# RWKV pair scores of a two-layer mixer trunk: ScalarE copies and a GpSimd select in place of VectorE's masked copies

## The chip, the core and the metric

The kernel runs on one core of a Trainium2 chip. The metric is the device time of one execution in microseconds, the median of several runs. A core has five engines that work side by side and wait for each other by semaphores: TensorE (PE in the rows, its weight loads PEld), VectorE (DVE), ScalarE (ACT), GpSimd (POOL) and SyncE (SP). Each engine takes its own instructions strictly in the order in which they stand in its queue, and DMAs are issued from the queues of SP and ACT here. An instruction that waits therefore holds up everything behind it on its engine.

## What is computed

The reference is a trunk of two layers on 256 positions of width 1024. Each layer normalises its input, projects it into the head groups of four token mixers (stick-breaking attention, RWKV-7, block attention, HGRN2), gates and sums their outputs, projects once more, and ends in a SwiGLU feed-forward part. The change touches RWKV-7 alone, whose recurrence is

```python
def step(state, inp):
    r_t, w_t, k_t, v_t, a_t, b_t = inp
    sa = jnp.einsum('bhvk,bhk->bhv', state, a_t)
    state = (state * w_t[:, :, None, :] + sa[..., None] * b_t[:, :, None, :]
             + v_t[..., None] * k_t[:, :, None, :])
    return state, jnp.einsum('bhvk,bhk->bhv', state, r_t)
```

for four heads of 64. The kernel computes it in two chunks of 128 positions. In a chunk, every pair of an earlier position s and a later position t has a score for each head: two tables, LB from b and LK from k, each against a (pairs s < t) and against r (pairs s <= t). Pairs outside these triangles count as zero. From LB a triangular system is solved, first in blocks of 16.

## The kernel before

All matrix products of the projections are made in three passes over a high and a low part: `split` (lines 127 to 129) makes the high part of a weight tile by a cast on ACT (`hi`) and the low part by a subtraction on DVE (`lo`). TensorE takes one weight tile of 128x1024 after another; four such pairs fit (`spl=4`), so a cast waits until TensorE has finished with the pair four tiles back.

The function `drive` interleaves the projections with two streams of mixer work by a planned TensorE clock: stream 0 is `rwkv`, stream 1 is `sba`, `moba` and `hgrn` in turn. The order on TensorE follows from that plan. On the other engines a scheduler sets the order from the dependences as it sees them.

Inside `rwkv` the part that matters runs like this, in each layer:

- `pair_scores` (line 534) is called four times: for LB of chunks 0 and 1, then LK of chunks 0 and 1. It makes eight small matmuls into two PSUM tiles `p1` (two buffers in all, so the next call's matmuls wait until the tiles before are read), two heads in each. A memset on GpSimd has zeroed the target `dst` (128 rows s, four heads, 256 columns: 128 for a, 128 for r), and line 542 lets DVE copy only the pairs in the triangle, by the 0/1 mask `armask`.
- `send` (line 547) writes the a half of LB to `flat` in HBM by a DMA from ACT's queue (line 548). Line 564, also from ACT's queue, reads the 16x16 diagonal blocks back as `xb` (tile `h`) when both writes have landed.
- Lines 570 to 594, on DVE, invert these blocks in `yb`. Line 599 writes `yb` to `tri` in HBM and line 602 reads it back spread over all partitions, both from ACT's queue. Line 602 waits until the write has landed.

At the same time TensorE runs the last projection of HGRN (`hgrn_proj`, function `use_n`, lines 809 to 813): two PSUM tiles `pa`, each emptied by a copy and a sigmoid on ACT (lines 810 and 811) and a product on DVE (line 812). There are three `pa` buffers. The gate unit that follows takes the third one and then needs the first of these two back, so its matmuls wait for line 812.

Of the kernel before, what the change touches and what calls it, by code (L numbers as in the profile page):

```python
# [15 lines left out]
OP = mybir.AluOpType  # L16
# [30 lines left out]
def trunk(ctx, tc, x, w_t, w_n, w_br, w_out, w_gu, w_dn, par, lora, rows, gains, consts, masks, out):  # L47
    nc = tc.nc
# [8 lines left out]
    def sb(tag, width, dt=F32):  # L57
        return mx.tile([128, width], dt, name=tag, tag=tag, bufs=NB[tag])

    def ps(tag):  # L60
        return psum.tile([128, 512], F32, name=tag, tag=tag, bufs=NB[tag])

    def g2d(t, a):
        return t.rearrange("p (a t) -> p a t", a=a)
# [4 lines left out]
    def over(t, n):  # L69
        return t[:, None, :].to_broadcast([128, n, t.shape[-1]])  # L70
# [3 lines left out]
    def mm(o, l, r, start=True, stop=True):  # L74
        n = 1
        for d in r.shape[1:]:
            n *= d
        m = l.shape[-1]
        pe[0] += max(m / 1.2, n / 2.4) if r.dtype == F32R else max(m / 0.6, n / 0.6)
        nc.tensor.matmul(o, l, r, start=start, stop=stop)  # L80
# [134 lines left out]
    armask = mk[:, 0:256]  # L215
# [220 lines left out]
    def head_sums(q, tag):  # L436
        p = ps(tag)
        for t in range(2):
            for hp in range(2):
                mm_cols(p[:, t * 4 + hp * 2:t * 4 + hp * 2 + 2], q[:, hp, t * 128:(t + 1) * 128], blk2)  # L440
        return p
# [4 lines left out]
    def hrow(a):  # L446
        return slice((a % 2) * 64, (a % 2) * 64 + 64)
# [17 lines left out]
    def rwkv(m, l, yT):  # L465
# [43 lines left out]
        p = head_sums(sq, "p1")  # L509
# [8 lines left out]
        p = ps("p1")  # L518
# [14 lines left out]

        def pair_scores(src, dst, c):
            p = [ps("p1"), ps("p1")]
            nc.gpsimd.memset(dst, 0.0)
            for a in range(4):
                hp = a // 2
                mm(p[a % 2][:, hp * 256:(hp + 1) * 256], src[hrow(a), hp, c * 128:(c + 1) * 128],
                   AR[hrow(a), 2 * hp + c].rearrange("p u t -> p (u t)"))  # L540
            for u in range(2):
                nc.vector.copy_predicated(dst[:, u::2], over(armask, 2), g2d(p[u], 2))  # L542

        flat = dram.tile([8, 128 * 129], F32, name="flat")
        tri = dram.tile([64, 256], F32, name="tri")
# [5 lines left out]
        for c in range(2):  # L551
            LB.append(g2d(sb("b1", 1024), 4))
            pair_scores(bn, LB[c], c)
            yield 1600
            send(c)
# [10 lines left out]
        for c in range(2):  # L566
            LK.append(g2d(sb("b1", 1024), 4))
            pair_scores(kh, LK[c], c)
            yield 3200
# [49 lines left out]
        for c in range(2):  # L619
            z5 = z[c].rearrange("p a (b u h) -> p a b u h", u=2, h=16)  # L620
            p = ps("p1")
# [4 lines left out]
        for c in range(2):  # L626
            p = ps("p1")
# [12 lines left out]
        p = [ps("p1"), ps("p1")]  # L640
# [6 lines left out]
        p = [ps("p1"), ps("p1")]  # L647
# [11 lines left out]
        for c in range(2):  # L659
            z6.append(g2d(sb("h1", 256), 4))  # L660
            p = ps("p1")
# [4 lines left out]
        for c in range(2):  # L666
            zs.append(g2d(sb("h1", 256), 4))
            p = ps("p1")
# [5 lines left out]
        for c in range(2):  # L674
            p = ps("p1")
# [6 lines left out]
        if l:  # L682
            p = ps("p1")
# [11 lines left out]
        p = ps("p1")  # L695
# [6 lines left out]
        p = ps("p1")  # L702
# [10 lines left out]
        p = head_sums(rx, "p1")  # L713
# [7 lines left out]
        p = ps("p1")  # L721
# [8 lines left out]
        for c in range(2):  # L730
            p = ps("p1")
# [9 lines left out]
            p = ps("p1")  # L741
# [3 lines left out]
            u = sb("h1", 256)  # L745
            nc.scalar.copy(u, p[:, 0:256])
            yield 1000
            if c == 0:
                p = ps("p1")
# [12 lines left out]
            p = ps("p1")  # L762
# [533 lines left out]
```

## Time and profile before

| | us |
|---|---|
| median of 3 runs | 926.57 (925.06 to 928.9) |
| the profiled execution | 930.03 |
| its span, first to last instruction | 928.2 |
| TensorE busy in the span | 910.3 |
| DVE, ACT, GpSimd busy | 651.4, 475.5, 83.8 |
| mean granted TensorE clock | 0.996 |

TensorE is the engine to look at: only what makes it wait, or what it waits for, can move the time. The second layer repeats the first one; in the place of this change it does so 452.6 us later (the write of `tri` is issued at 112.19 and at 564.75 us). The rows below come from the stretch around 80 to 120 us and its twin in the second layer.

### The profile page before, as it was taken

To read this page: it belongs to the slowest core of one execution; us is meant where nothing else is said; L and a number is where in the kernel's file an instruction comes from. 1 tells how busy PE (TensorE), PEld (TensorE's weight loads), DVE (VectorE), ACT (ScalarE), POOL (GpSimd) and SP (SyncE) were. 2 spreads that over 40 slices of the span, in tenths; PEclk is the share of its full clock that TensorE was granted. 3 is DMA by queue.
4 is the path that set the end of the run, shared out by engine and by line. 5 is a ranking of instruction groups with operands and counts; after the bars stand their busy time and mean duration, and the time that the engine had idled before them with its cause. 6 is when DMAs were issued, how large, how long until landed. Compare 5 with 4: busy or idle time off the path is not lost.

```text
span 928.2 us, 14996 instructions
## 1 busy us (share of the span) xinstructions
PE 910.3 (98%) x5902; PEld 761.5 (82%) x5902; DVE 651.4 (70%) x957; ACT 475.5 (51%) x726; POOL 83.8 (9%) x94
## 2 busy tenths in 40 slices
PE   8999899999999999999999998999999999999996
PEld 5999678778888888888889986767787888888885
DVE  5668877786766666677567778768678566666665
ACT  5564385445535545456445645644455345555453
POOL 3001100323000000000000201023130000000000
PEclk9999999999999999999999999999999999999999
DMA  8654454345864556568435444533368356666551
GB/s 302 204 159 137 130 175 136 114 147 166 256 220 134 183 183 184 182 206 272 155 114 161 159 140 127 186 103 115 119 208 264 114 181 204 185 182 201 181 181 46
DMA packets 50424, 158.11 MB, mean 170 GB/s; under 512 B 9393, under 2 KB 11953, under 8 KB 50354
## 3 DMA queue, kind: packets, MB, share of 16 engines
q1 hardware_dynamic: 43632, 155.19, 52.4%
q10 hardware_dynamic: 6722, 1.97, 0.9%
q8 instruction: 46, 0.75, 0.3%
q14 instruction: 24, 0.20, 0.1%
HBM read 154.91 MB, written 2.23 MB: 169 GB/s over the span
## 4 chain that ended last, share of the span: by engine, by line
PE 80%; DVE 10%; DMA 4%; issue 2%; ACT 2%; POOL 0%; SPq 0%; ACTq 0%; POOLq 0%; DVEq 0%
PE pa L80 56%; PE p L80 23%; DVE lo L129 2%; PE p L89 1%; PE pa L89 1%; DMA h<-flat 1%; DMA xr<-in_x_dram 1%; DVE b L542 1%; DMA flat<-b 1%; DVE xy L591 1%; DMA raw<-in_w_n_dram 1%; DMA lora<-in_lora_dram 1%; DMA raw<-in_w_gu_dram 1%; DVE b L867 1%; DVE b L965 1%
## 5 line engine op out<-in xcount | busy, mean ns | idle before, releaser
L129 DVE TENSOR_TENSOR lo<-raw,hi 128x1024 fp32r<-128x1024 f32 x268 | 331.0, 1240 | 153.6 <-ACT hi L128 150.6
L128 ACT CAST hi<-raw 128x1024 fp32r<-128x1024 f32 x268 | 279.2, 1048 | 225.5 <-PE pa L80 107.4
L80 PE MATMUL pa<-h,hi 128*128 128x256 f32 (+1 forms) x1280 | 277.9, 339 | 0.0
L80 PEld LDWEIGHTS pa<-h,hi 128*128 128x128 f32 x1280 | 215.9, 190 | 24.6 <-issue 2.0
L80 PE MATMUL pa<-hi,h 128*128 128x512 f32 x576 | 194.1, 402 | 4.6 <-DVE p L812 4.6
L80 PE MATMUL pa<-h,lo 128*128 128x256 f32 x960 | 179.9, 283 | 0.0
L80 PEld LDWEIGHTS pa<-h,lo 128*128 128x128 f32 x960 | 148.6, 191 | 7.0 <-issue 0.7
L80 PEld LDWEIGHTS pa<-hi,h 128*128 128x128 f32 x576 | 109.0, 189 | 31.5 <-DVE p L812 5.5
L80 PE MATMUL pa<-lo,h 128*128 128x512 f32 x288 | 113.6, 394 | 0.0
L80 PE MATMUL p<-hi,c 128*128 128x512 f32 (+1 forms) x352 | 113.4, 394 | 0.0
L80 PEld LDWEIGHTS p<-hi,c 128*128 128x128 f32 x352 | 66.1, 189 | 15.2 <-DVE c L129 0.6
L80 PE MATMUL p<-lo,c 128*128 128x512 f32 (+1 forms) x176 | 69.2, 393 | 0.0
L80 PEld LDWEIGHTS pa<-lo,h 128*128 128x128 f32 x288 | 54.5, 189 | 9.9
L263 POOL TENSOR_TENSOR rs<-rs,half 128x1 f32<-128x1 f32 x10 | 6.0, 597 | 471.6 <-DVE rs L262 471.6
L80 PE MATMUL pa<-hi,y 128*128 128x512 f32 x128 | 44.0, 399 | 0.1
L80 PE MATMUL p<-hi,b 128*128 128x512 f32 x128 | 41.4, 396 | 0.2 <-DVE b L129 0.2
L80 PEld LDWEIGHTS p<-lo,c 128*128 128x128 f32 x176 | 33.1, 188 | 6.8
L1033 POOL TENSOR_TENSOR p<-p,gt 128x512 f32<-128x512 f32 x16 | 30.9, 1953 | 39.4 <-DVE gt L1031 31.8
L340 DVE TENSOR_TENSOR gt<-gt,pa 128x256 f32<-128x256 f32 x80 | 33.2, 414 | 0.0
L128 ACT CAST c<-xy 128x512 fp32r<-128x512 f32 x20 | 12.4, 620 | 39.2 <-DVE xy L1136 39.2
L339 ACT COPY gt<-pa 128x256 f32<-128x256 f32 x80 | 29.3, 366 | 0.0
L80 PEld LDWEIGHTS pa<-hi,y 128*128 128x128 f32 x128 | 24.0, 188 | 6.3 <-issue 0.7
(276 smaller groups left out, 943.4 us busy)
## 6 DMA issues: line engine op xcount, KB each, us to landing
raw<-in_w_gu_dram SPq DMA_DIRECT2D x88, 512.0 KB, 3.9
raw<-in_w_n_dram SPq DMA_DIRECT2D x80, 512.0 KB, 3.6
raw<-in_w_dn_dram SPq DMA_DIRECT2D x44, 512.0 KB, 3.5
raw<-in_w_t_dram SPq DMA_DIRECT2D x40, 512.0 KB, 3.5
raw<-in_w_br_dram SPq DMA_DIRECT2D x16, 512.0 KB, 4.0
raw<-in_w_out_dram SPq DMA_DIRECT2D x16, 512.0 KB, 4.4
b<-in_gains_dram SPq DMA_DIRECT2D x4, 512.0 KB, 5.5
flat<-b ACTq DMA_DIRECT2D x4, 256.0 KB, 3.2
```

The costliest lines, as they stand in the source:

```text
L80: nc.tensor.matmul(o, l, r, start=start, stop=stop)
L89: nc.tensor.transpose(o, i, ident)
L128: a = nc.scalar.copy(dst[0], src)
L129: return a, (eng or nc.vector).tensor_tensor(dst[1], src, dst[0], op=OP.subtract)
L263: nc.gpsimd.tensor_tensor(dst, dst, half[:, :dst.shape[-1]], op=OP.pow)
L339: nc.scalar.copy(dst, p[:, 256:512])
L340: nc.vector.tensor_tensor(dst, dst, p[:, 0:256], op=OP.add)
L542: nc.vector.copy_predicated(dst[:, u::2], over(armask, 2), g2d(p[u], 2))
L591: nc.vector.tensor_tensor(pr[:, b, i], l4[:, b, i, None].to_broadcast(bc), r.to_broadcast(bc), op=OP.mult)
L867: nc.vector.tensor_tensor(qv, qv, t4[s, :, :, 0:1].to_broadcast([64, 2, 2 * nb, hb]), op=OP.mult)
L965: nc.vector.tensor_tensor_scan(kb, kb, reset[t][:, ::-1], 1.0, op0=OP.mult, op1=OP.add)
L1033: e.tensor_tensor(mg[f, t], mg[f, t], g, op=OP.add)
```

## The change

The memset goes. After the matmuls, ACT copies both PSUM tiles whole into `dst`, and GpSimd then goes over `dst` in place, once for the a half and once for the r half. Its select computes (column - row + u - 1) from the indices, keeps the element where that is not negative, and writes 0.0 elsewhere: s < t for u = 0, s <= t for u = 1.

```diff
         def pair_scores(src, dst, c):
             p = [ps("p1"), ps("p1")]
-            nc.gpsimd.memset(dst, 0.0)
             for a in range(4):
...
             for u in range(2):
-                nc.vector.copy_predicated(dst[:, u::2], over(armask, 2), g2d(p[u], 2))
+                nc.scalar.copy(dst[:, u::2], g2d(p[u], 2))
+            for u in range(2):
+                v = dst[:, :, u * 128:(u + 1) * 128]
+                nc.gpsimd.affine_select(v, v, [[0, 4], [1, 128]], OP.is_ge, 0.0, base=u - 1, channel_multiplier=-1)
```

In two layers with four calls each that is 16 masked copies on DVE and 8 memsets on GpSimd less, 16 copies on ACT and 16 selects on GpSimd more. Lines after 542 of the changed kernel are numbered two higher. TensorE's instructions and their order stay as they were; on the other engines the scheduler places some of the neighbours anew.

The first place is ACT's queue around the two writes of LB. `b1_953` is LB of chunk 0, `b1_1000` (in the changed kernel `b1_1001`) of chunk 1, `p1_...` their PSUM tiles, and what an instruction waits for stands in brackets. Before:

```order
L960 ACTIVATE b2_944<-b2_933 128x1024 [waits DVE_49]
L961 ACTIVATE b2_933<-b2_933 128x1024 [waits Activation_49]
L128 CAST hi_1113<-raw_1111 128x1024 [waits DMAHW4_49,PE_49]
L548 DMA flat_951<-b1_953 128x4x128 [waits DVE_49,Pool_49]
L548 DMA flat_951<-b1_1000 128x4x128 [waits DVE_49,Pool_49]
L796 COPY p_1022<-pa_916 128x512 [waits PE_49]
```

And in the changed kernel:

```order
L962 ACTIVATE b2_944<-b2_933 128x1024 [waits DVE_49]
L541 COPY b1_953<-p1_954 128x2x256 [waits PE_49]
L963 ACTIVATE b2_933<-b2_933 128x1024 [waits Activation_49]
L541 COPY b1_953<-p1_955 128x2x256 [waits PE_49]
L128 CAST hi_1115<-raw_1113 128x1024 [waits DMAHW4_49,PE_49]
L550 DMA flat_951<-b1_953 128x4x128 [waits Pool_49]
L541 COPY b1_1001<-p1_1002 128x2x256 [waits PE_49]
L541 COPY b1_1001<-p1_1003 128x2x256 [waits PE_49]
L550 DMA flat_951<-b1_1001 128x4x128 [waits Pool_49]
L798 COPY p_1024<-pa_916 128x512 [waits PE_49]
```

Both writes now wait for GpSimd, and the copies of chunk 1 stand behind the first of these waits.

The second place is ACT's queue around the write and the read of `tri`; `pa_1109` and `pa_1110` (in the changed kernel `pa_1111` and `pa_1112`) are the PSUM tiles of HGRN's last projection. Before:

```order
L128 CAST hi_1282<-raw_1280 128x1024 [waits DMAHW1_49,PE_49,Activation_49]
L128 CAST hi_1300<-raw_1298 128x1024 [waits DMAHW4_49,DVE_49,PE_49]
L128 CAST hi_1318<-raw_1316 128x1024 [waits DMAHW5_49,DVE_49,PE_49]
L599 DMA tri_952<-yb_118 64x256 [waits DVE_49]
L810 COPY p_1107<-pa_1109 128x256 [waits PE_49]
L811 ACTIVATE p_1108<-pa_1109 128x256
L602 DMA h1_1372<-tri_952 128x8x16 [waits DMAHW3_49,DMAHW1_49]
L810 COPY p_1107<-pa_1110 128x256 [waits PE_49]
```

And in the changed kernel:

```order
L128 CAST hi_1286<-raw_1284 128x1024 [waits DMAHW1_49,DVE_49,PE_49]
L541 COPY b1_1181<-p1_1182 128x2x256 [waits PE_49]
L541 COPY b1_1181<-p1_1183 128x2x256 [waits PE_49]
L601 DMA tri_952<-yb_118 64x256 [waits DVE_49]
L128 CAST hi_1304<-raw_1302 128x1024 [waits DMAHW4_49,PE_49,Activation_49]
L604 DMA h1_1376<-tri_952 128x8x16 [waits DMAHW0_49]
L128 CAST hi_1322<-raw_1320 128x1024 [waits DMAHW5_49,PE_49,Activation_49]
L812 COPY p_1109<-pa_1111 128x256 [waits PE_49]
L813 ACTIVATE p_1110<-pa_1111 128x256
L812 COPY p_1109<-pa_1112 128x256 [waits PE_49]
```

Two casts moved from before the write of `tri` to behind it, and the read of `tri` moved ahead of the first copy out of `pa`.

The third place is the end of the inversion on DVE, up to line 812. Before:

```order
L129 TENSOR_TENSOR lo_1283<-raw_1280,hi_1282 128x1024
L591 TENSOR_TENSOR xy_1249<-yb_118,h1_1120 64x512
L594 TENSOR_REDUCE h1_1250<-xy_1249 64x64
L542 COPY_PREDICATED b1_1178<-mk_116,p1_1179 128x2x256
L542 COPY_PREDICATED b1_1178<-mk_116,p1_1180 128x2x256
L591 TENSOR_TENSOR xy_1249<-h1_1250,yb_118 64x512
L129 TENSOR_TENSOR lo_1301<-raw_1298,hi_1300 128x1024
L594 TENSOR_REDUCE yb_118<-xy_1249 64x8x8
L129 TENSOR_TENSOR lo_1319<-raw_1316,hi_1318 128x1024
L812 TENSOR_TENSOR p_1108<-p_1108,pa_1109 128x256
```

And in the changed kernel:

```order
L593 TENSOR_TENSOR xy_1253<-yb_118,h1_1122 64x512
L129 TENSOR_TENSOR lo_1287<-raw_1284,hi_1286 128x1024
L596 TENSOR_REDUCE h1_1254<-xy_1253 64x64
L593 TENSOR_TENSOR xy_1253<-h1_1254,yb_118 64x512
L596 TENSOR_REDUCE yb_118<-xy_1253 64x8x8
L129 TENSOR_TENSOR lo_1305<-raw_1302,hi_1304 128x1024
L129 TENSOR_TENSOR lo_1323<-raw_1320,hi_1322 128x1024
L814 TENSOR_TENSOR p_1110<-p_1110,pa_1111 128x256
```

The copies are gone, one subtraction less stands ahead of the last step of the inversion, and two that wait for the moved casts stand between it and the product of `use_n`.

## Rows read from the trace of the kernel before

**Rows 1.** The page: busy time by engine; the chain that ended last.

```profile
PE 910.3 (98%) x5902; PEld 761.5 (82%) x5902; DVE 651.4 (70%) x957; ACT 475.5 (51%) x726; POOL 83.8 (9%) x94
...
PE 80%; DVE 10%; DMA 4%; issue 2%; ACT 2%; POOL 0%; SPq 0%; ACTq 0%; POOLq 0%; DVEq 0%
```

**Rows 2.** Waits of TensorE: total us, times, longest us.

```profile
PE pa L80 <- DVE p L812: 4.6, 2, 2.3
...
PEld pa L80 <- DVE p L812: 5.5, 2, 2.8
```

**Rows 3.** Chain that ended last, first layer, by time: start us, us, what.

```profile
88.06 0.68 DVE b L542 x2
...
88.81 3.23 DMA flat<-b
...
92.12 3.92 DMA h<-flat
...
96.07 0.17 DVE yb L570
...
111.49 0.68 DVE yb L594
...
113.41 0.43 DVE p L812
...
113.89 4.22 PE pa L80 x11
```

**Rows 4.** ACT in order of time, both layers: start us, us.

```profile
82.26 1.06 ACT L961 ACTIVATE b<-b 128x1024 f32<-128x1024 f32 x1
...
94.79 1.07 ACT L938 COPY c<-p 128x512 f32<-128x512 f32 x2
...
112.19 0.49 ACTq L599 DMA_DIRECT2D tri<-yb  x1
...
115.33 0.38 ACTq L602 DMA_DIRECT2D h<-tri  x1
...
116.30 1.05 ACT L128 CAST hi<-raw 128x1024 fp32r<-128x1024 f32 x1
...
564.75 0.47 ACTq L599 DMA_DIRECT2D tri<-yb  x1
...
568.84 0.38 ACTq L602 DMA_DIRECT2D h<-tri  x1
```

**Rows 5.** DVE in order of time, during the inversion of the first layer.

```profile
100.47 1.33 DVE L542 COPY_PREDICATED b<-mk,p 128x512 f32<-128x512 uint8 x2
...
108.17 1.33 DVE L542 COPY_PREDICATED b<-mk,p 128x512 f32<-128x512 uint8 x2
...
110.35 1.21 DVE L129 TENSOR_TENSOR lo<-raw,hi 128x1024 fp32r<-128x1024 f32 x1
```

**Rows 6.** Stretches: PE, PEld, DVE, ACT, POOL busy; PEclk, DMA share, GB/s.

```profile
113.90:118.60 4.70, 4.70 (x14) 3.72 (x15) 3.10 (x6) 2.83 (x4) 2.36 (x3) 0.64 0.70 199
...
566.40:571.00 4.60, 4.57 (x20) 3.81 (x21) 2.03 (x6) 1.72 (x4) 1.28 (x2) 1.00 0.73 214
```

**Rows 7.** GpSimd's groups by shape: busy us, mean ns, idle before.

```profile
L1033 POOL TENSOR_TENSOR p<-p,gt 128x512 f32<-128x512 f32 x16 | 30.9, 1953 | 39.4 <-DVE gt L1031 31.8 <-DVE bs L715 7.6
...
L982 POOL TENSOR_TENSOR p<-p,cn 128x512 f32<-128x512 f32 x4 | 4.3, 1096 | 32.9 <-DVE c L980 32.9
...
L238 POOL MEMSET reset<- 128x512 f32 x2 | 1.0, 520 | 0.0
```

**Rows 8.** GpSimd, then DVE, in order of time where both work at once.

```profile
172.01 2.59 POOL L720 TENSOR_TENSOR c<-c,rws 128x256 f32<-128x256 f32 x2
...
174.92 1.41 DVE L868 TENSOR_TENSOR c<-c,tot 128x256 f32<-128x256 f32 x1
...
180.86 0.41 DVE L868 TENSOR_TENSOR c<-c,tot 128x256 f32<-128x256 f32 x1
```

**Rows 9.** Line 548 alone: ns min/median/max, first and last start.

```profile
L548 ACTq DMA_DIRECT2D flat<-b x4: 364/370/406, 85.3 to 541.5; - x4
```

## The prediction

> **What bounds the kernel now.** The page's first part comes first: TensorE is busy for 910.3 of 928.2 us, DVE for 651.4, GpSimd for 83.8 [rows 1]. So nothing that is taken off DVE counts as such; the question is only where TensorE waits, and for whom. The chain that ended last says the same, 80% TensorE, but leaves 10% to DVE and 4% to DMAs [rows 1]. TensorE's waits, read next, are nearly one single place: twice, once a layer, it waits 2.3 us for line 812 on DVE, 2.8 us as its weight loads show it [rows 2].
>
> The chain read by time through the first layer shows what stands behind that wait [rows 3]. It is the work of this change: the masked copies of LB's chunk 1 on DVE (88.06), its write to HBM (88.81, 3.23 us), the read back (92.12, 3.92 us), the inversion on DVE from 96.07 to 112.17, and then, only because ACT's queue is in order, the write of `tri` is issued at 112.19 [rows 4], lines 810 and 811 follow on ACT, line 812 on DVE takes 0.43 us, and TensorE goes on at 113.89. Lines 810 to 812 need nothing from RWKV. They stand behind the write. So the end is set here by when LB reaches HBM, how long the inversion takes, and what stands in ACT's queue between its end and line 810. I cost the change by these three terms. T is the duration of one select.
>
> **Term 1: the second write of LB.** Before, it is issued at 88.81, when DVE has made its copies [rows 3]. Now ACT makes them. Two copies of 512 columns out of PSUM take 1.07 us on ACT, 0.54 each [rows 4]. ACT is free at 82.26, where line 961 stands now [rows 4]: copy to 82.8, line 961 (1.06) to 83.85, copy to 84.4. Two selects end at 84.4 + 2T. ACT, waiting there, issues the first write (0.37 us, [rows 9]), and only then may copy chunk 1, 1.07 us; two more selects; the second write. With 0.1 us for the handing over between engines: 84.4 + 0.37 + 1.07 + 0.1 + 4T = 86.0 + 4T, against 88.81: **-2.8 + 4T**. Four selects stand in series, since the copies of chunk 1 are queued behind the wait for chunk 0. Behind the second wait stand a copy out of `pa` and casts of weights; TensorE needs them several us later, and what it would lose there it would otherwise lose at line 812, so I count nothing for them.
>
> **What T is.** No select is in the trace. From below, a memset of 512 columns takes 0.52 us on GpSimd, and it only writes; from above, a product of 512 columns in place with two inputs takes 1.10 us, and another 1.95 us in the mean, where DVE works beside it [rows 7]. A select reads one input, makes an index, compares, and writes in place: nearest to the 1.10. I take T = 1.0 and keep 0.52 and 1.95 as ends. So term 1 is +1.2 us (-0.7 to +5.0).
>
> **Term 2: the inversion.** From the arrival of the blocks to its last step DVE also makes the two pairs of copies of LK, 100.47 to 101.70 and 108.17 to 109.40 (1.23 each by the start of what follows), and a subtraction of 1.14 (1.21 by its row) at 110.35, which the scheduler now puts behind the end [rows 5]. These go: **-3.6**. The four copies of LK now on ACT come after chunk 1's casts and do not wait for GpSimd; TensorE needs their tiles free only at the next pair of scores, several us later: nothing.
>
> **Term 3: from the end of the inversion to TensorE.** Before it is 113.89 - 112.17 = 1.7 us [rows 3]. Now the read of `tri` and two casts stand ahead of line 810 (812 of the changed kernel), and the read waits until the write has landed. From the issue of the write to that of the read it is 115.33 - 112.19 = 3.1 us in the first layer and 568.84 - 564.75 = 4.1 us in the second [rows 4]. Then the read's issue 0.38, the cast 1.05 [rows 4], the subtraction that waits for this cast on DVE ahead of the product 1.2 [rows 5], the product 0.43 [rows 3], handing over 0.1: 6.3 and 7.3 us. The other moved cast lies under the landing. **+4.6 and +5.6**. The landing could not be hidden: until line 812 TensorE has only the first few matmuls of the gate unit.
>
> **Term 4: the shared way into SBUF.** Where GpSimd works on SBUF data, a DVE product of 256 columns took 1.41 us instead of 0.41 [rows 8]: one GpSimd instruction held one of DVE's up for 1.0 us. The memset of before had been out of the way; four selects on LK now fall into the inversion, and those on LB beside a scan and a product. Bounds: 0, or every one of the four holding up the inversion for T, 4.0 us, and about 1 us more on LB. In rows 8 two instructions of GpSimd cost that product 1.0 us, so 0.5 each; four selects make 2.0, less for those that come while DVE does what isn't held up. I take **+1.5** a layer. The Trainium skill (SBUF — State Buffer, Who interferes with whom) says that a DVE instruction with two SBUF inputs and a GpSimd instruction that reads SBUF exclude each other, the later waiting for the whole of the earlier, while one that only writes doesn't contend. The trace agrees by the 1.0 us above; by that rule, with every select coming first, the term would lie at its upper bound, 5.0, and the sum 3.5 us higher in each layer.
>
> **Term 5: the clock.** After the 2.3 us wait the granted clock was 0.64 in the mean over 4.7 us in the first layer, so for most of it at the lower level, 1.2 GHz; after the same wait in the second layer it was 1.00, 2.4 GHz throughout [rows 6]. The wait now becomes some 6 us in both, so I count the first layer's loss, 4.7 x 0.36 = 1.7 us, for the second too. It could also stay away (0).
>
> **The sum.** First layer 1.2 - 3.6 + 4.6 + 1.5 = 3.7, second 4.7, clock 1.7: **+10.1 us**. With T left open it is 8T + 2.1; T alone, from 0.52 to 1.95, moves it from +6.3 to +17.7. Against the profiled execution, 930.03 becomes 940.1; that execution lies 3.5 above the median, and on the median 926.57 it is 936.7. I forecast **936.7**.
>
> What DVE gains elsewhere (16 copies of 0.62 in all, 9.9 us) and what ACT takes on (16 of 0.54, 8.6 us) I count as nothing: TensorE's largest wait is the one for line 812 [rows 2], and what makes TensorE earlier ahead of it only brings it to that wait sooner.
>
> **Rivals.** *The select is cheap (not slower).* If T is 0.52 as for the memset, and it keeps out of DVE's way, the second write goes out 0.7 earlier, and terms 1 to 3 are -0.7 - 3.6 + 4.6 = +0.3 and +1.3: with no clock lost +1.6, 928.2 on the median, within 0.5%. For: GpSimd's one-input rows are the memsets alone, at 1 ns a column. Against: it must also read and compare. With nothing lost to DVE and to the clock the sum is 8T - 2.6, so this rival decides for T below 0.9, where that stays under 4.6. The Trainium skill (GPSIMD Engine Reference, Engine selection) calls one-input work on GpSimd roughly line-rate and only two-input work about twice as slow as DVE. That is this rival's price; no row here shows a one-input instruction that reads.
>
> *The select is slow.* At 1.95 us, as the products under DVE's load, the sum is 10.1 + 8 x 0.95 = +17.7, 944.3. For: the selects stand beside DVE's work just as those products do. Against: at LB's second pair DVE has little to do.
>
> *The wait goes (faster).* If the inversion ended so early that all of term 3 lay under TensorE's own work, both waits and the first layer's slow clock would vanish: 2 x 2.3 + 1.7 = 6.3 us less, 920.3. TensorE comes to the wait at 113.89 - 2.3 = 111.6 [rows 2, 3], so the inversion would have to end by 111.6 - 6.3 = 105.3, 6.9 earlier than now. For: DVE is rid of four copies there, and the write of LB may go out sooner. Against: terms 1 and 2 give 4.3 at the cheapest select.
>
> **How the numbers follow.** Forecast 0.55; cheap select 0.25; slow select 0.15; no wait 0.05. What a measurement of this kernel can tell from no change is about 0.5%, 4.6 us. Slower takes the forecast and the slow select, faster the last case, same the cheap select: 0.70, 0.25, 0.05. The range reaches from just under the cheap select, 927.0, to just over the slow one, 947.0.
>
> **What would show it.** The selects' mean in GpSimd's groups (1.0; below 0.6 is the first rival); the second write of LB at about 90.0; `yb`'s last step at about 111.3 with term 4; the read of `tri` ahead of the first copy out of `pa` on ACT; TensorE's wait for the product of `use_n` at 5 to 8 us each instead of 2.3, still twice; and the clock below 1.00 after it in both layers. I am wrong if that wait doesn't grow, or if TensorE shows a new wait elsewhere of that size.

## The result, and the profile after

The changed kernel takes **934.04 us** (median of 6 runs, 933.08 to 936.28) against 926.70 for the kernel before in runs beside it (6 runs, 924.74 to 928.90). The ratio is 1.0078, 95% interval 1.0061 to 1.0095: **7.3 us slower**, 936.7 was forecast. Line numbers behind 545 are higher by 2 than in the kernel before.

The page of the kernel after, its busy times and its chain that ended last, to be read against [rows 1]:

```profile
PE 908.6 (98%) x5902; PEld 760.9 (82%) x5902; DVE 648.8 (70%) x941; ACT 484.0 (52%) x742; POOL 94.6 (10%) x102
...
PE 83%; DVE 8%; DMA 3%; issue 2%; ACT 1%; POOL 1%; ACTq 0%; POOLq 0%; DVEq 0%
```

DVE lost 2.6 us of work, not 9.9: what is left slows down. TensorE has the same instructions. Its waits (total us, times, longest us), to be read against [rows 2], hold the difference in one line:

```profile
PE pa L80 <- DVE p L814: 9.7, 2, 5.1
...
PEld pa L80 <- DVE p L814: 10.6, 2, 5.5
```

The same wait as before, twice, now 4.7 and 5.1 us instead of 2.3 each. The chain that ended last, read by time through the first layer (start us, us, what), is the one of [rows 3] with two new links, GpSimd's selects ahead of the write to `flat`, and the landing of `tri` behind the inversion:

```profile
78.37 1.06 ACT b L962
...
81.41 2.40 POOL b L544 x2
...
84.02 1.38 POOL b L544
85.42 4.24 DMA flat<-b
...
89.74 3.31 DMA h<-flat
...
93.07 0.17 DVE yb L572
...
107.41 0.69 DVE yb L596
108.12 1.96 DMA tri<-yb
...
111.55 0.37 ACT p L812
...
112.82 0.42 DVE p L814
...
113.29 8.93 PE pa L80 x31
```

ACT in order of time behind the inversion's end (start us, us; in brackets how long it was idle ahead, and for whom):

```profile
108.73 1.04 ACT L128 CAST hi<-raw 128x1024 fp32r<-128x1024 f32 x1 [7.58 <-DVE yb L596]
110.10 0.38 ACTq L604 DMA_DIRECT2D h<-tri  x1
110.60 1.04 ACT L128 CAST hi<-raw 128x1024 fp32r<-128x1024 f32 x1 [0.82 <-DMA tri<-yb]
111.55 0.37 ACT L812 COPY p<-pa 128x256 f32<-128x256 f32 x1
```

Write of `tri`, cast, read, cast, and only then the first copy out of `pa`. The new selects and, below them, the older products beside which they run, in GpSimd's groups (busy us, mean ns); then the spread of the selects when the trace is asked for their tile (ns min/median/max, first and last start); last, the second select of chunk 1 alone (start us, us):

```profile
L544 POOL TENSOR_SCALAR_AFFINE_SELECT b<-b 128x512 f32<-128x512 f32 x16 | 16.2, 1039 | 1.2 <-ACT b L541 1.2
...
L984 POOL TENSOR_TENSOR p<-p,cn 128x512 f32<-128x512 f32 x4 | 5.2, 1315 | 22.0 <-DVE c L982 22.0
...
L544 POOL TENSOR_SCALAR_AFFINE_SELECT b<-b x16: 632/1084/1614, 81.4 to 557.9; 128x512 f32<-128x512 f32 x16
...
85.34 0.63 POOL L544 TENSOR_SCALAR_AFFINE_SELECT b<-b 128x512 f32<-128x512 f32 x1
```

T was taken as 1.0 and is 1.04 in the mean. But it is no single duration: the select at 85.34, with nothing running on DVE, took 0.63, and most of those beside DVE's steps with two inputs took 1.08 to 1.61. Last, TensorE alone by stretch (us, busy, granted clock, DMA share, GB/s): the four stretches of 4 us behind its resumes, before and then after.

```profile
113.89:117.89 4.00, 4.00 (x11) 0.63 0.82 234
117.89:121.89 4.00, 4.00 (x18) 0.95 0.42 132
566.43:570.43 4.00, 4.00 (x18) 1.00 0.74 234
570.43:574.43 4.00, 4.00 (x19) 1.00 0.27 71
```

```profile
113.29:117.29 4.00, 4.00 (x11) 0.57 0.68 224
117.29:121.29 4.00, 4.00 (x19) 1.00 0.44 131
569.08:573.08 4.00, 4.00 (x9) 0.50 0.60 203
573.08:577.08 4.00, 4.00 (x16) 0.81 0.40 131
```

Half clock is 0.50, so the kernel before lost 4 x (0.37 + 0.05) = 1.7 us in the first layer and nothing in the second; the changed one 1.7 and 4 x (0.50 + 0.19) = 2.8.

The spans of single traces are not compared, because the first layer's stage begins at 78.4 to 79.5 us in 5 of the 13 kernels traced here and at 81.2 in the other 8, whichever the kernel. **All marks below are therefore counted from the start of ACT's first sigmoid of the stage**, line 960 before (81.17 and 533.84 us) and 962 after (78.37 and 533.86). For first / second layer:

| kernel | second write to `flat` | `yb` begun | inversion, us | its end | end to resume, us | TensorE resumes | time against before, 95% |
|---|---|---|---|---|---|---|---|
| before | 7.64 / 7.64 | 14.90 / 14.78 | 16.1 / 16.1 | 30.99 / 30.88 | 1.7 / 1.7 | **32.72 / 32.59** | 1 |
| after | 7.05 / 7.03 | 14.70 / 15.02 | 15.0 / 15.0 | 29.72 / 30.05 | 5.2 / 5.2 | **34.92 / 35.22** | 1.0061 to 1.0095 |
| after, read later | 7.04 / 7.03 | 14.62 / 14.70 | 15.0 / 15.0 | 29.63 / 29.72 | 4.5 / 4.4 | 34.09 / 34.16 | 1.0048 to 1.0094 |
| after, casts first | 7.04 / 7.03 | 15.02 / 14.97 | 15.1 / 15.1 | 30.07 / 30.04 | 2.7 / 2.7 | 32.72 / 32.69 | 0.9984 to 1.0020 |
| after, other half first | 8.31 / 8.26 | 16.54 / 15.83 | 14.7 / 14.9 | 31.21 / 30.72 | 3.6 / 3.6 | 34.80 / 34.28 | 1.0047 to 1.0093 |
| after, no selects on LK | 7.03 / 7.03 | 14.88 / 15.03 | 13.7 / 13.7 | 28.62 / 28.76 | 5.2 / 5.2 | 33.81 / 33.92 | 1.0031 to 1.0064 |
| after, GpSimd reads nothing during the inversion | 7.03 / 7.02 | 14.89 / 14.82 | 12.3 / 12.3 | 27.23 / 27.17 | 5.2 / 5.2 | 32.42 / 32.34 | 0.9976 to 1.0010 |
| LK only | 7.64 / 7.64 | 14.87 / 14.84 | 14.7 / 14.7 | 29.52 / 29.50 | 5.6 / 5.5 | 35.08 / 35.01 | 1.0076 to 1.0105 |
| LK only, casts first | 7.65 / 7.64 | 15.08 / 14.96 | 14.7 / 14.7 | 29.78 / 29.66 | 2.7 / 2.7 | 32.43 / 32.31 | 0.9974 to 1.0007 |
| LB only | 8.85 / 8.86 | 17.04 / 17.30 | 18.2 / 18.2 | 35.28 / 35.51 | - | 34.08 / 34.31 | 1.0015 to 1.0044 |
| LB only, memsets later | 7.04 / 7.03 | 14.84 / 15.18 | 16.0 / 16.1 | 30.86 / 31.23 | 1.7 / 1.7 | 32.60 / 32.94 | 0.9998 to 1.0033 |
| before, late product | 7.64 / 7.64 | 14.77 / 14.82 | - | 34.05 / 34.13 | - | 30.81 / 30.88 | 0.9936 to 0.9964 |
| after, late product | 7.03 / 7.03 | 14.86 / 15.18 | - | 34.04 / 34.33 | - | 30.78 / 31.07 | 0.9938 to 0.9964 |

(A dash: TensorE resumes ahead of the inversion's end. The runs of the table are explained in the next section.)

### The profile page after: what moved, and what is told of

Its sections match the earlier page's. It is cut to its first block, busy times and chain, and to the rows that moved or that the text cites. A ratio compares the mean times of both kernels' runs of the same rounds, so it can differ in the third digit from the quotient of the medians.

```text
span 931.8 us, 14998 instructions
## 1 busy us (share of the span) xinstructions
PE 908.6 (98%) x5902; PEld 760.9 (82%) x5902; DVE 648.8 (70%) x941; ACT 484.0 (52%) x742; POOL 94.6 (10%) x102
## 3 DMA queue, kind: packets, MB, share of 16 engines
q10 hardware_dynamic: 6722, 1.97, 0.9%
## 4 chain that ended last, share of the span: by engine, by line
PE 83%; DVE 8%; DMA 3%; issue 2%; ACT 1%; POOL 1%; ACTq 0%; POOLq 0%; DVEq 0%
PE pa L80 58%; PE p L80 23%; DVE lo L129 2%; PE pa L89 1%; PE p L89 1%; DMA flat<-b 1%; DMA h<-flat 1%; DMA raw<-in_w_n_dram 1%; DVE xy L593 1%; POOL b L544 1%; DMA raw<-in_w_gu_dram 1%; DVE b L869 1%; DMA tri<-yb 0%; PE pa L196 0%; DVE c L129 0%
## 5 line engine op out<-in xcount | busy, mean ns | idle before, releaser
L80 PE MATMUL pa<-hi,h 128*128 128x512 f32 x576 | 196.2, 406 | 9.7 <-DVE p L814 9.7
L80 PEld LDWEIGHTS pa<-lo,h 128*128 128x128 f32 x288 | 55.3, 192 | 10.1
```

## The experiments

The kernel before had medians of 927.71, 927.19 and 928.35 us beside the three sets of runs, about 1 us above the 926.7 from which the expectations were worked out, so ratios are compared and not times.

The theory after the comparison: the loss is ACT's queue behind the inversion's end (+3.5 us a layer) with the half clock that follows the longer wait; the inversion's gain (1.1 instead of 3.6 less) was eaten by GpSimd reading SBUF beside DVE; the way of LB over GpSimd costs nothing. The rivals are that the selects on the way to `flat`, or ACT's and GpSimd's added work as such, carry it.

### Behind the inversion's end: the read of `tri`, and the casts

Read later (in the changed kernel; `sig` collects the sigmoids of `use_n`):

```diff
-        nc.scalar.dma_start(cb, bass.AP(tensor=tri.tensor, offset=tri.offset, ap=[[16, 128], [2048, 8], [1, 16]]))
...
+        with tc.issue_after(sig[2 * l].ins):
+            nc.scalar.dma_start(cb, bass.AP(tensor=tri.tensor, offset=tri.offset, ap=[[16, 128], [2048, 8], [1, 16]]))
```

> The changed kernel with one move: the read of tri is issued behind the first sigmoid of use_n instead of ahead of ACT's second cast, so that ACT no longer stands still until the write of tri has landed. Theory (the cost is ACT's queue behind the inversion's end): the read costs what the trace of the changed kernel shows as waited for ahead of that cast, 0.82 us, and the casts and the second subtraction stay in the way; TensorE resumes about 0.9 us earlier in each layer, 112.4 instead of 113.3 in the first, and the median falls from 934.0 to about 932. Rival (the cost is a later second write of LB, or the lock of GpSimd on DVE): the resume moves with nothing else, and the time stays within 0.5 us of 934.0 only if something behind the read then ends last.

Casts first (the write of `tri`, and with it the read, goes behind the second sigmoid):

```diff
-        nc.scalar.dma_start(tri.rearrange("p (s t) -> p s t", s=16), yb)
...
+        with tc.issue_after(sig[2 * l + 1].ins):
+            nc.scalar.dma_start(tri.rearrange("p (s t) -> p s t", s=16), yb)
```

> The changed kernel with one move: the write of tri, and with it the read, is issued behind use_n's second sigmoid, so that both casts and both pairs of copies out of pa stand ahead of it on ACT. Theory (ACT's queue): what is left behind the inversion's end is DVE's two subtractions (1.1 to 1.2 each) and the product (0.42), about 2.8 us to TensorE's resume instead of 5.2, so 2.4 us less in each layer, and about 1 more if the clock stays up in the second layer: 928 to 929.5. What then remains against the kernel before, 1.5 to 3 us, would be the price of two subtractions in place of one. Rival (the later half of the change, selects and lock, carries the loss): the stall falls but the time stays above 932.

Measured: read later 933.77 us, ratio 1.0071 (1.0048 to 1.0094); its resume is 0.83 and 1.06 us earlier, as expected, but the time, for which about 932 was expected, can't be told from that of the whole change. Casts first 927.05, below the 928 to 929.5 expected, ratio **1.0002 (0.9984 to 1.0020): the whole loss is gone**, with nothing left over for the second subtraction, and TensorE resumes where it does in the kernel before. Putting the same instructions on ACT's queue in another order was worth 7 us. TensorE's wait, and the chain behind the inversion's end, in the kernel with casts first:

```profile
PE pa L80 <- DVE p L816: 4.8, 2, 2.5
```

```profile
108.13 0.04 DVE yb L596
...
108.73 2.34 DVE lo L129 x2
111.07 0.34 DVE p L816
```

So of the 3.5 us between the inversion's end and the resume the read was about 0.7 (5.2 to 4.5 and 4.4 in the table), the wait for the casts 1.8 (down to 2.7), and the last 1.0 is the second subtraction itself, which stays. (The rest of the 0.83 and 1.06 is an earlier start of `yb`.) And it shows what the shorter inversion was worth: two subtractions now stand between its last step and the product where one stood before, and the resume is at 32.7 all the same. The subtraction taken out of the inversion was only moved behind it. With this order the granted clock stayed at 1.00 behind both waits of 2.4 us.

### The selects on the way to `flat`

Other half first:

```diff
-            for u in range(2):
+            for u in (1, 0):
                 v = dst[:, :, u * 128:(u + 1) * 128]
...
```

> The changed kernel with the two selects of each tile in the other order: the half with u=1 first, then u=0, the half that goes to flat. Each write of LB then waits for both selects of its tile, the second one for all four, as the prediction had reckoned; in the changed kernel it waits for three. Theory (that is why the prediction's first term was too high by 1.8 us): the second write comes about 1.0 to 1.4 us later, at least one select, the inversion and the resume move with it in each layer, and the time is 936 to 937. Rival (the write is set by something else, or the inversion has slack in front): the write moves by less than 0.5 us, or the inversion's end doesn't move, and the time is 934.

Measured 933.29, ratio 1.0070 (1.0047 to 1.0093). The second write goes out 1.26 and 1.23 us later, at 8.3: in the changed kernel it does wait for three selects and not for four. The time does not follow, so the expectation of 936 to 937 failed. In this kernel the scheduler placed one more cast ahead of the inversion's end on ACT, where it stands at 102.92 in order of time:

```profile
102.92 1.06 ACT L128 CAST hi<-raw 128x1024 fp32r<-128x1024 f32 x1
...
112.52 0.37 ACT L812 COPY p<-pa 128x256 f32<-128x256 f32 x1 [0.74 <-DMA tri<-yb]
```

Behind the end it is 3.6 us then instead of 5.2. TensorE also waits 1.6 us at a new place in the first layer, for ACT's copies of line 940. As a measurement of what a later write costs the run is inconclusive; as a second one of ACT's queue it agrees.

### What GpSimd does to the inversion

No selects on LK (`bn` is the source of LB):

```diff
-                nc.gpsimd.affine_select(v, v, [[0, 4], [1, 128]], OP.is_ge, 0.0, base=u - 1, channel_multiplier=-1)
+                if src is bn:
+                    nc.gpsimd.affine_select(v, v, [[0, 4], [1, 128]], OP.is_ge, 0.0, base=u - 1, channel_multiplier=-1)
+                else:
+                    nc.gpsimd.memset(v, 0.0)
+                    nc.gpsimd.memset(v, 0.0)
```

> The changed kernel with the four selects on LK in each layer replaced by memsets of the same halves, two for each, so that GpSimd is about as long at work there but only writes; LK becomes zero, so that part of the scores is left out. Theory (reading and writing by GpSimd slows DVE's steps with two inputs beside it): the inversion, 15.0 us from its first step to its last in the changed kernel, shortens to 12.5 to 13, the resume comes 2 to 2.5 earlier in each layer, and the time is 929 to 930. Rival (the inversion is as long because of its own chain or of DVE's other work, and the select's kind doesn't matter): it stays at 15 and the time at 934.

GpSimd reads nothing during the inversion (the same, and at line 984; the selects on LB, ahead of the inversion, stay):

```diff
-            nc.gpsimd.tensor_tensor(g2d(u, 2), g2d(u, 2), over(cosT, 2), op=OP.mult)
+            nc.gpsimd.memset(u, 0.0)
```

> The changed kernel without the selects on LK (memsets in their place, as in the experiment before this) and with the line-984 products on GpSimd replaced by memsets of their tile as well, so that GpSimd reads nothing while the inversion runs; LK and the line-984 products are left out. Theory (GpSimd's reading and writing beside DVE's two-input steps is what took back the gain of the inversion): the pair of line-983 products on DVE, 2.68 us in the changed kernel, takes 1.25 to 1.3, the inversion 12.3 to 12.5 instead of 15.0 with all selects and 13.7 without those on LK, so that all of the 3.6 us of work taken out of it shows; resume 32.4 to 32.6, time 928 to 930 because the tail of 5.2 and the half clock stay. Rival (something else holds those products): they stay at 2.6 and the inversion at 13.7.

Measured: the inversion takes 13.7 us without LK's selects (12.5 to 13 was expected: only half of it) and **12.3 us where GpSimd only writes** (expected 12.3 to 12.5). Times: 932.36, ratio 1.0047 (1.0031 to 1.0064), above the 929 to 930 expected since the inversion gained only half as much; and 927.27, ratio 0.9993 (0.9976 to 1.0010), a little below the 928 to 930 expected: with the resume back at 32.4 the wait is 2.1 and 2.2 us, and the clock stayed at 1.00 behind both. In this run ACT's order is still that of the changed kernel, with 5.2 us behind the inversion's end. So the whole loss goes by either of two edits, casts first or no reads by GpSimd, and their shares don't add up: each alone brings the wait back to the length it had before. DVE in order of time (start us, us), the pair of products at line 983 and the two at 985, in the changed kernel, then the same two in the last one:

```profile
97.29 2.68 DVE L983 TENSOR_TENSOR c<-c,cn 128x512 f32<-128x512 f32 x2
99.89 1.11 DVE L985 TENSOR_TENSOR c<-c,p 128x512 f32<-128x512 f32 x1
...
101.53 1.10 DVE L985 TENSOR_TENSOR c<-c,p 128x512 f32<-128x512 f32 x1
```

```profile
98.03 1.27 DVE L987 TENSOR_TENSOR c<-c,cn 128x512 f32<-128x512 f32 x2
99.23 0.67 DVE L989 TENSOR_TENSOR c<-c,p 128x512 f32<-128x512 f32 x1
...
100.43 0.67 DVE L989 TENSOR_TENSOR c<-c,p 128x512 f32<-128x512 f32 x1
```

And what GpSimd does meanwhile, in the changed kernel and in the last one:

```profile
96.83 2.59 POOL L984 TENSOR_TENSOR p<-p,cn 128x512 f32<-128x512 f32 x2 [10.86 <-DVE c L982]
99.38 3.76 POOL L544 TENSOR_SCALAR_AFFINE_SELECT b<-b 128x512 f32<-128x512 f32 x4
```

```profile
97.54 1.17 POOL L988 MEMSET p<- 128x512 f32 x2 [11.03 <-DVE c L986]
98.66 0.99 POOL L547 MEMSET b<- 128x512 f32 x2
```

While GpSimd writes only, each of DVE's products takes 0.64 to 0.67. While it reads, each is held up by 0.4 to 0.7. Of the 2.7 us that GpSimd costs the inversion, the selects on LK make 1.3 and the two products at line 984 the other 1.4. Those products are old. In the kernel before (GpSimd's row, then DVE's) they ran beside the first pair of masked copies of LK [rows 5] and only one product of DVE, 0.99 us long; with the copies gone, both of DVE's products moved up to where they are:

```profile
100.00 2.15 POOL L982 TENSOR_TENSOR p<-p,cn 128x512 f32<-128x512 f32 x2 [16.52 <-DVE c L980]
```

```profile
101.70 0.99 DVE L981 TENSOR_TENSOR c<-c,cn 128x512 f32<-128x512 f32 x1
```

### One half of the change at a time

LB only (`new = src is bn`; LK only with `is not`):

```diff
+            if not new:
+                nc.gpsimd.memset(dst, 0.0)
...
-                nc.scalar.copy(dst[:, u::2], g2d(p[u], 2))
-            for u in range(2):
+                if new:
+                    nc.scalar.copy(dst[:, u::2], g2d(p[u], 2))
+                else:
+                    nc.vector.copy_predicated(dst[:, u::2], over(armask, 2), g2d(p[u], 2))
+            for u in range(2 * new):
```

> The change made for LB alone: LB is copied by ACT and masked by GpSimd, LK as in the kernel before by a memset and DVE's masked copies. ACT's order then has both casts and the copies out of pa ahead of the write of tri. Theory (the loss sits in ACT's queue behind the inversion's end, and the LB half costs nothing, since its second write waits for three selects and comes 0.6 us sooner than before): landing 8.0, inversion about 16.1 (both pairs of masked copies back in it), tail 1.7 as before, so TensorE resumes 32.6 to 33.0 after the start of ACT's first sigmoid, as in the kernel before (32.7 and 32.6), and the time is 926.5 to 929. Rival (GpSimd's selects on the way to flat carry the loss): at least half of it is there, 930 or more.

> The change made for LK alone: LB by a memset and DVE's masked copies as in the kernel before, LK by ACT and GpSimd. ACT's order then has the write and the read of tri ahead of the second cast and the copies, as in the whole change. Theory (the loss sits there): landing and second write as before, inversion 15.0, tail 5.2, TensorE resumes 34.9 to 35.2 after the start of ACT's first sigmoid against 32.6 before, and the time is 932 to 935, nearly all of the loss. Rival (the LB half carries it): below 930.

LK only: 936.51 (4 runs), ratio **1.0090 (1.0076 to 1.0105)**, a little above the 932 to 935 expected and all of the loss, with 5.5 us from the inversion's end to the resume and the same wait of 4.8 us in each layer. LB only: 930.36, ratio 1.0030 (1.0015 to 1.0044), 926.5 to 929 expected: a miss. GpSimd in order of time shows why:

```profile
84.23 2.39 POOL L550 TENSOR_SCALAR_AFFINE_SELECT b<-b 128x512 f32<-128x512 f32 x2 [0.39 <-ACT b L545]
86.58 1.84 POOL L538 MEMSET b<- 128x1024 f32 x2
88.37 2.23 POOL L550 TENSOR_SCALAR_AFFINE_SELECT b<-b 128x512 f32<-128x512 f32 x2
```

```profile
PE p L80 <- ACT c L946: 3.9, 2, 2.0
...
PE pa L80 <- DVE p L820: 1.4, 2, 0.7
```

LK's memsets (the first fence), which the whole change doesn't have, stand between LB's selects and hold the second write back by 1.8 us. ACT, which stands at the read of `flat` until that write has landed, then comes later to the copies of line 946, and TensorE waits 2.0 us a layer for them and 0.7 for the product of `use_n` (the second fence: total us, times, longest us). The experiment had made a cost of its own. So it was repeated with one more edge, here against the first form, `sel` being the list of the selects:

```diff
             if not new:
-                nc.gpsimd.memset(dst, 0.0)
+                with tc.issue_after(sel[-1].ins):
+                    nc.gpsimd.memset(dst, 0.0)
```

> The change for LB alone again, with LK's two memsets on GpSimd issued behind the last select on LB; in the first form of this experiment they stood between the selects and held the second write back, from 7.0 to 8.9 after the start of ACT's first sigmoid. The order of ACT behind the inversion is that of the kernel before. Theory (the LB half costs what its landing costs and no more): second write at 7.0, yb begun at 14.9 to 15.2 against 14.8 to 14.9 before, inversion about 16.1, tail 1.7, resume 32.6 to 33.0, time 926.5 to 928.5. Rival (the way over GpSimd to flat carries a loss of its own): 929.5 or more, as in the first form.

And LK only got the order with the casts first (the edit of that run, on LK only):

> The change for LK alone, and the write of tri issued behind use_n's second sigmoid, so that casts and copies stand ahead of it on ACT. Theory (of the 8 to 9 us of LK alone all is ACT's queue behind the inversion's end): yb begun at 14.85, inversion 14.65, tail 2.65 as in the whole change with the same order, resume 32.1 to 32.2 against 32.6 to 32.7 before, the clock at 1.00 behind both: 924.5 to 927. Rival (GpSimd's selects beside DVE, or ACT's four more copies, carry a loss of their own): 930 or more.

Measured: LB only 929.08, ratio 1.0016 (0.9998 to 1.0033), its time slightly above the range expected and not to be told from no change; resume at 32.60 and 32.94, as expected. LK only with casts first 927.81, ratio 0.9991 (0.9974 to 1.0007), where 924.5 to 927 was expected: the loss is gone, and nothing gained (behind the first layer's wait of 2.2 us the granted clock was 0.68 over 4 us, which the expectation had put at 1.00). As rivals to ACT's order both fall: once that order is right, neither LB's way over GpSimd nor the added work on ACT and GpSimd, with DVE's copies gone, costs time that these runs can tell from nothing (for LB up to 0.3% is not excluded). While the order is as in the changed kernel, GpSimd's reads do cost time, as the two runs of the section before show.

### Taking the inversion out of TensorE's way

The last experiment goes at what both kernels wait for: the inversion's last step on DVE (product and sum) is issued behind the first product of `use_n`, in both kernels alike (here `sig` collects DVE's products):

```diff
+            if lev < 3:
+                product(blk(yb, 0, 1), t4, blk(yb, 1, 1))
+        yield 4000
...
+        with tc.issue_after(sig[2 * l + 0].ins):
             product(blk(yb, 0, 1), t4, blk(yb, 1, 1))
-        yield 4000
+        yield 100
```

> The kernel before with one move: the inversion's last step on DVE (the second product of lev 3 and its sum, 1.03 and 0.68 us) is issued behind use_n's first product, so that tri is written later and TensorE's wait for a pa tile no longer ends behind the inversion. ACT then has both pairs of copies ahead of the write. Theory (what TensorE waits for at this place is use_n's product and nothing of the inversion): the wait falls by 1.03 + 0.68 = 1.7 us in each layer, from 2.3 to about 0.6, and the clock stays at 1.00 behind it, another 1.7 in the first layer: about 5 us less than the kernel before, 922 to 923. Rival (the later tri is waited for in its turn, by the products with Y): no gain, 926 to 928.

> The changed kernel with the same move: the inversion's last step behind use_n's first product, casts and copies of ACT ahead of the write of tri. Theory: what remains of the change once nothing of the inversion stands in TensorE's way is nothing: DVE has 2.5 us less of masked copies in each layer, but the subtractions and the lock take it back; the resume comes 1.7 us before the one with casts and copies ahead of the write (32.7 after the start of ACT's first sigmoid), at about 31.0, and the time is 922 to 924, the same as for the kernel before with this move within 0.2%. Rival (the change has a gain of its own that the wait had hidden): 2 us or more below the kernel before with this move.

Measured: **923.55 us, ratio 0.9950 (0.9936 to 0.9964)**, and **923.18, ratio 0.9951 (0.9938 to 0.9964)**. Both are faster than the kernel before, and so than the changed one, by the same amount; the first came out 0.6 us above its range, the second within. TensorE's wait, in the kernel before and in the changed one, each with this move:

```profile
PE pa L80 <- DVE p L817: 1.1, 2, 0.5
```

```profile
PE pa L80 <- DVE p L819: 1.3, 2, 0.9
```

The rival, a wait for the later `tri` in its turn, shows nowhere among TensorE's waits; the only new one there is 1.3 us for a cast at line 128, in the first of the two kernels alone. Once the inversion is out of the way, the change makes no difference that these runs can tell.

## Why the prediction was right, and where it was not

Direction and size came out, 7.3 us slower against 10.1 reckoned, and the place was the one named. The sum was 2.5 us too high, with errors of both signs in it. By its terms, from the table, for first / second layer:

| term | predicted | measured |
|---|---|---|
| 1, second write of LB | +1.2 / +1.2 | -0.6 / -0.6 |
| write to `yb` begun | not in the sum | +0.4 / +0.9 |
| 2 and 4, inversion and shared way | -2.1 / -2.1 | -1.1 / -1.1 |
| 3, its end to TensorE | +4.6 / +5.6 | +3.5 / +3.5 |
| TensorE's resume | +3.7 / +4.7 | +2.2 / +2.6 |
| 5, clock in the second layer | +1.7 | +2.8 |
| sum of both layers | +10.1 | +7.6; by the medians +7.3 |

Of the signs named, the selects' mean, the place of the read of `tri`, `yb`'s last step (111.3 is 30.1 by these marks; 29.7 and 30.1 came) and the clock below 1.00 in both layers came as said. That `yb`'s last step came in its place is luck: term 1 was 1.8 us too high, while term 4 was 1.0 too low and the longer way to `yb`, 0.4 and 0.9, was not in the sum, and these errors cancel. The second write was early (8.8 by these marks, 7.0 came), and the waits were 4.7 and 5.1 us where 5 to 8 was said.

**Term 1 was too high by 1.8 us, and the step that failed is "four selects stand in series".** Only the half with u=0 goes to `flat`, and each write waits for the one select that makes it. So chunk 0's second select runs while ACT is already issuing and copying. Three selects stand ahead of the second write on GpSimd, and only two of them count in time, since the second one ends before ACT's copies of chunk 1 do: with two, the prediction's own sum gives 86.0 + 2T = 88.0, 0.8 us before the old 88.81, and 0.6 came. T was right in the mean, though not for the reason given: it is 0.63 with DVE idle and mostly 1.08 to 1.61 beside DVE's steps with two inputs. With the halves in the other order, where each write does wait for both selects, the write came 1.2 us later, most of the 1.8. Against that, the way from the write to `yb` got longer by 0.4 and 0.9 us, which the sum had left out. In the first layer the write to `flat` took 1.0 us longer to land (4.24 instead of 3.23) and the read 0.6 less (3.31 instead of 3.92); no run settled why.

**Term 2 was right in what it took out; term 4 was mis-sized, 2.5 us instead of 1.5.** Its rate was misread from [rows 8]: the two instructions of line 720 end at 174.60, before the product at 174.92 begins, and what runs beside that product is one other instruction of GpSimd, line 1033 from 174.56 to 176.04. So one instruction cost 1.0, not two 0.5 each. In GpSimd's order of time:

```profile
174.56 1.48 POOL L1033 TENSOR_TENSOR p<-p,gt 128x512 f32<-128x512 f32 x1
```

Without any reads by GpSimd the inversion is 3.8 us shorter than before (16.1 against 12.3), close to the 3.6 of term 2 and the 0.3 by which the product at line 981 had been held up. For the selects alone the 1.5 was near, they cost 1.3, but with that rate this was luck. What it missed is that taking work out of DVE's row brings other two-input steps of DVE beside GpSimd work that was there already. The rule cited, that GpSimd reading SBUF and a DVE step with two SBUF inputs exclude each other while writes don't contend (the Trainium skill, SBUF — State Buffer, Who interferes with whom), fits the three runs: the same pair took 2.68 us in the changed kernel, 2.67 without LK's selects, and 1.27 where GpSimd only writes. The extreme reckoned by it, 5.0 us a layer, did not come.

**Term 3 was the right mechanism with one size off.** The landing of `tri` took 1.98 and 1.95 us instead of the 3.1 and 4.1 read from [rows 4]. What differs is the traffic beside it: the kernel before moved 214 and 224 GB/s in those stretches, the changed one 143 and 137. First layer, before and then after (us; PE, PEld, DVE, ACT, POOL busy; granted clock, DMA share, GB/s):

```profile
112.19:115.33 3.14, 1.44 (x5) 1.19 (x6) 2.95 (x6) 0.66 (x2) 0.74 (x1) 0.93 0.78 214
```

```profile
108.12:110.10 1.98, 0.50 (x3) 0.07 (x1) 0.29 (x1) 1.04 (x1) 0.00 (x0) 1.00 0.41 143
```

That less traffic made it faster would fit these two kernels, but other traces speak against it as the only cause: in LK only the same write landed in 2.35 and 2.29 us at 232 and 209 GB/s, and in the run with the other half first in 1.97 and 1.95 at 33 and 34. The cause stays open. The term's claim that the landing "could not be hidden" held for this order; the run with the read moved shows it was worth 0.7 us, less than the casts.

**Term 5 was right in kind.** The second layer lost its clock as well, 2.8 us rather than 1.7.

**The rivals.** The cheap select fails at T: 1.04, above the 0.9 from which it would decide. The roughly line-rate for one input (the Trainium skill, GPSIMD Engine Reference, Engine selection) is not refuted by these selects: with DVE idle one took 0.63 us for 512 columns, against 0.52 for a memset. It is beside DVE that the mean rose to 1.04, so it was the other half of the rival's condition, that the select keeps out of DVE's way, that failed. The slow select fails at the same row. The vanishing wait didn't come by the change, but the last two runs made it come, at 923.2 to 923.6 rather than 920.3, with 0.4 to 0.9 us of each wait left. That DVE's relief elsewhere is worth nothing held: with the wait gone, both kernels take the same time.

## What to carry to other kernels

When an edit moves work between engines, look at what the scheduler then puts into an in-order queue between the bottleneck's release and what it waits for; here, with two casts and a read in front of a copy, a kernel lost 7 us, and one ordering edge gave all of it back. That an edit gives all of a loss back does not make it the only cause: taking GpSimd's reads out of the inversion did so too. Before costing a chain of handed-over steps, find which of them each wait names: a consumer of one half waits for one half. And an experiment that undoes half of a change must be looked at for instructions that stand in a new place, as the memsets between the selects did.

## What the runs showed of the hardware

A select by index on GpSimd, 512 columns of fp32 in place, took 0.63 us with DVE idle and up to 1.61 beside DVE's steps with two inputs. GpSimd reading and writing SBUF held up DVE's two-input steps of 512 columns from 0.67 to 1.1 or 1.34 us each; GpSimd's memsets in the place of its selects and products held up none.

TensorE's clock fell to the half level behind every wait of 3.2 us or more at this place (10 of 10, in five kernels; 0.50 to 0.69 in the mean of the 4 us behind it), behind 2 of 10 waits of 2.1 to 2.5 us (0.63 and 0.68), and behind none of the six of 0.9 us or less. So a wait that grows from 2.3 to 5 us costs more than its length: where the clock fell, 1.6 to 2.8 us of work were lost behind it.
